# Inverse copies by rows, two local banks, planned slack for small matmuls, and a reordered first tile in a hybrid encoder step

## The chip, the cores and the metric

The kernel runs on one core of a Trainium2 chip. The metric is the device time of one execution in microseconds (us), as the median over several runs; lower is better. Five engines work side by side and meet at semaphores: TensorE (PE) multiplies matrices and loads its weights through PEld; VectorE (DVE), ScalarE (ACT) and GpSimd (POOL) do the elementwise work; SyncE (SP) issues the DMAs. PE writes its results into eight PSUM banks of 128x512 float32 numbers, and DVE and ACT read them from there.

## The reference

One layer of a hybrid encoder over 2048 prompt tokens and 32 sample tokens, width 1024. After a normalisation, a projection feeds two mixers; their outputs are projected back, and a feed-forward layer follows.

```
h = rmsnorm(x) * (1 + scale1) + shift1          # scale, shift, gate from silu(c) @ ada_w
p = h @ w_in                                    # columns: u, v | q, k, v | z | a, b
mixer A:  out = u * (W_s rmsnorm(v) + b_s)      # per chunk of 128 positions
mixer B:  gated delta rule, 4 heads x 128, in chunks:
    lmat = (kb k^T) * decay + I
    u_c, w_c = triangular_solve(lmat, ...)      # the inverse
    per chunk: v_new = u_c - w_c S;  o = qg S + attn v_new;  S = S * gl + kg^T v_new
x += gate1 * (concat(A, B) @ w_out)
x += gate2 * (relu(h2 @ w_up)^2 @ w_down);  y = rmsnorm(x)
```

## The kernel before

**A planner sets the order.** The kernel writes its operations into a list (`Program.op`), each with its engine, an estimated cost, and the operations that it must follow. `Program.schedule` then plays the list through: at each step the engine that is free first takes its best ready operation. What comes out is a fixed order for each engine; no time of the plan reaches the chip. Each engine works through its order and waits at semaphores where an operand is not there. Priorities go CHAIN, INV, LOCAL, EVAC, GEMM, IDLE. On PE everything but GEMM is small, and a dictionary `HOLD` lets GEMM matmuls pass a ready small one for a while: before the change LOCAL alone is held, by 1000 planned ns. Costs between engines are in `LATENCY`.

**Stages.** The tokens go in two halves of 1024 and 1056, each cut in groups of up to 512 columns. A projection tile (`gemm`) is 24 matmuls into one bank: eight slices of the contraction, each as three products (high by high, high by low, low by high parts of float32). The stages: `startup` (x is loaded, its sum of squares gives the row of inverse roots r, the modulation comes from `ada_first`, and h is made tile by tile for the first group while z is projected); then for each half `v_stage`, eight slabs of projection weights, with the delta rule beside them, and `u_stage`; then `out_stage` for both halves; then `feed_forward`.

**Banks.** `self.banks` gives tags to the eight banks: "g" (0, 1, 2) for projection tiles, "L" (3) for the local work of the delta rule, "C" (4, 5) for its chain over chunks, "B" (6) for the inverse, "M" (7) for sums, transposes and the gating mixer. The feed-forward part uses all eight as "f". Each use of a tag takes the next bank of its ring and must follow the last reader of that bank.

**The delta rule.** For each half and head, `delta_local` makes the matrices of each chunk pair (bank L), `delta_inv` the inverse: eight or ten small copies take the 16x16 diagonal blocks out to a DRAM tensor `nd_d`, one load brings them back in another shape, POOL inverts them all at once in 30 operations, two or four copies go through `ud_d`, and six sets of small matmuls (bank B) put the blocks together. `delta_chain` then walks over the chunks with two heads side by side; in each chunk PE works three times (`pa`, `px`, `pu`, bank C), with DVE or ACT between, and each step needs the one before.

**What the planner knows of the DRAM copies.** A view's region is that of the slice it was made from; `re(...)` keeps it. Before the change all copies into `nd_d` are views of `nd[:64]` rearranged, and so each overlaps the others and follows them in the plan, with `DMA_LATENCY` (3500 planned ns) between.

**The start.** In `startup`, `stats(0)` ends in `rms_row`: PE sums the squares into bank M, DVE and POOL take the power of -0.5, PE spreads the result over the partitions into bank M, and ACT copies it to a row in SBUF. Each first tile is then multiplied by the row (`h_value`; for every third k on POOL), scaled, split into BH and BL, and used. `consts` sets constants on POOL with `fill`.

Of the kernel before, what the change touches and what calls it, by code (L numbers as in the profile page):

```python
# [11 lines left out]
ALU = mybir.AluOpType  # L12
# [44 lines left out]

CHAIN, INV, LOCAL, EVAC, GEMM, IDLE = range(6)
TURN = 84
HOLD = {LOCAL: 1000}  # L60

# [133 lines left out]
def R(x):  # L195
    return x.ap if isinstance(x, View) else x
# [10 lines left out]
class Program:  # L207
# [37 lines left out]
    def schedule(self):  # L245
# [20 lines left out]
        def finish(i, start, end):  # L266
            o = ops[i]
            o.start = start
            order.append((start, i))
            for j in o.succ:  # L270
                s = ops[j]
                s.ready = max(s.ready, end + o.lat + LATENCY.get((o.eng, s.eng), 0.0))
                s.npred -= 1
                if s.npred == 0:
                    release(j, s.ready)
# [61 lines left out]
class Kern:  # L337
# [50 lines left out]
        e = self._e(eng)  # L388
        self.p.op(eng, c, lambda: e.tensor_copy(R(out), R(in_)), [out], [in_])

    def fill(self, out, value, eng=POOL):
        e = self._e(eng)
        self.p.op(eng, 100 + out.n, lambda: e.memset(R(out), value), [out], [])

    def transpose32(self, out, in_):
        nc = self.nc
# [152 lines left out]
    def setup(self):  # L549
# [108 lines left out]
    def startup(self):  # L658
        i, c = self.i, self.dma
        c(self.craw, i["cT"])  # L660
        self.act(self.cs, self.craw, AF.Silu)
        self.fill(self.ones, 1.0, DVE)
        self.fill(self.mhalf, -0.5, DVE)
        xr = [[8, 9, 10, 11], [4, 5, 7, 12]]
        x = [[self.slot(s, lo, (P, 512)) for s in xr[g] for lo in (0, HALF)] for g in range(2)]
        load = lambda g: [c(x[g][k], self.x_src(0)(k, 512 * g, 512)) for k in range(KT)]
        row = [self.row[:, 512 * g : 512 * g + 512] for g in range(2)]

        def stats(g):
# [12 lines left out]
        self.cp(self.nrm, k1[:, 96:120].re("p (n k) -> p n k", n=3))  # L682
        self.cp(self.ident, k1[:, 120:248])
        stats(0)
# [19 lines left out]
        self.consts()  # L704

    def consts(self):
        i = self.i
        ld = lambda v, src: self.dma(v, src, 4 * int(np.prod(v.shape)))
        bc = lambda v, n: self.dma(v, i[n].partition_broadcast(P))
        with self.p.at(GEMM):  # L710
            ld(self.wsT, i["wsT"])
            self.fill(self.wsT[64:128, :, 0:64], 0.0)
            bc(self.sgub, "sgub")
            bc(self.sgug, "sgug")
            ld(self.triu, i["triu"])
            ld(self.mask, i["mask"])
            ld(self.convw, i["convw"])
            ld(self.sconv, i["sconv"])
            ld(self.dngc, i["dngc"])
            bc(self.dtb, "dtb")  # L720
            bc(self.alog, "alog")
            for h in range(H):
                self.fill(self.S[h], 0.0)
            self.fill(self.halo, 0.0)
            self.fill(self.ab, 0.0)
            zero = self.slot(4, 0, (P, 1024))[:36]
            self.fill(zero, 0.0)
            for d in self.ud_d:
                self.dma(d.re("c a x -> (c a) x"), zero)
            self.fill(self.z0, 0.0)  # L730

            for x in self.r1s + self.vns + self.ofs:
                self.fill(x, 0.0)
            zero = self.slot(4, 0, (P, 384))
            self.fill(zero, 0.0)
# [116 lines left out]
        self.tt(bl, x, bh.f32(), ALU.subtract, eng)  # L852

    def h_value(self, hf, g, k, x, r, a, kind):
        self.tt(x, x, r, ALU.mult, POOL if k % 3 == 2 else DVE)
        for so, sw, q in segs(hf, g):
            s = slice(so, so + sw)
            c, b = a[:, k, q : q + 1], self.modc[:, kind, k, q : q + 1]
            if k % 4 == 1 and not kind:
                self.ts(x[:, s], x[:, s], c, ALU.mult, b, ALU.add, POOL)  # L860
            elif kind or k % 4 == 3:
                self.act(x[:, s], x[:, s], AF.Identity, scale=c, bias=b)
            else:
                self.ts(x[:, s], x[:, s], c, ALU.mult, b, ALU.add)
# [311 lines left out]
    def delta_inv(self, hf, h, nb):  # L1176
# [24 lines left out]
        ud_d = self.ud_d[self.nud % 2]  # L1201
        self.nud += 1
        for s in range(2):
            d = ud_d[:8].re("c a (s j t i) -> s t (c a) j i", s=2, j=16, t=2)
            self.dma(d[s, s], Uv[32 * s : 32 * s + 32])
            if hf == 1:
                d = ud_d[8:9, 0:1].re("c a (s j t i) -> s t (c a) j i", s=2, j=16, t=2)
                self.dma(d[s, s], Uv[64 + s : 65 + s])
# [448 lines left out]
    def put(self, ops, name, m, x):  # L1657
        ops.setdefault(name, {})[m] = self.operand(self.rp, x)
# [238 lines left out]
```

## Time and profile before

| | |
|---|---|
| median of 3 runs | 2337.24 us (2336.88 to 2339.47) |
| the profiled execution | 2330.84 us, of which the span 2328.8 us |
| granted TensorE clock | 0.998 |
| busy: PE, PEld | 98%, 93% of the span |
| busy: DVE, ACT, POOL | 71%, 53%, 26% |

The span goes from the first to the last instruction. An engine's busy time counts overlapping instructions once; a matmul's end is modelled, and one matmul begins before the one ahead of it has ended, so a PE that is busy may still begin its matmuls later than it could. The weight load (PEld) of a matmul stands in a row of its own, and a wait of PE for an operand shows there first.

### The profile page before, as it was taken

To read this page: it belongs to the slowest core of one execution; us is meant where nothing else is said; L and a number is where in the kernel's file an instruction comes from. 1 tells how busy PE (TensorE), PEld (TensorE's weight loads), DVE (VectorE), ACT (ScalarE), POOL (GpSimd) and SP (SyncE) were. 2 spreads that over 40 slices of the span, in tenths; PEclk is the share of its full clock that TensorE was granted. 3 is DMA by queue.
4 is the path that set the end of the run, shared out by engine and by line. 5 is a ranking of instruction groups with operands and counts; after the bars stand their busy time and mean duration, and the time that the engine had idled before them with its cause. 6 is when DMAs were issued, how large, how long until landed. Compare 5 with 4: busy or idle time off the path is not lost.

```text
span 2328.8 us, 45703 instructions
## 1 busy us (share of the span) xinstructions
PE 2292.2 (98%) x15906; PEld 2171.0 (93%) x15906; DVE 1653.2 (71%) x3651; ACT 1226.1 (53%) x2816; POOL 607.5 (26%) x830
## 2 busy tenths in 40 slices
PE   7999999999999999999999999999999999999998
PEld 4877879999999888999999999999999999999998
DVE  5557646667655546589999989776668886666775
ACT  5465546666655435376556555753344564334343
POOL 2235331332423323345544424200000250000001
PEclk9999999999999999999999999999999999999999
DMA  9789666657557767888777786997667797666771
GB/s 322 224 291 317 222 183 214 188 166 232 165 157 225 242 204 232 262 290 277 248 255 251 256 280 229 344 321 233 221 214 252 264 302 232 221 214 215 246 225 54
DMA packets 367247, 552.59 MB, mean 237 GB/s; under 512 B 70988, under 2 KB 191200, under 8 KB 367016
## 3 DMA queue, kind: packets, MB, share of 16 engines
q1 hardware_dynamic: 367016, 549.68, 72.5%
q8 instruction: 125, 2.05, 0.4%
q14 instruction: 106, 0.87, 0.1%
HBM read 395.25 MB, written 154.28 MB: 236 GB/s over the span
## 4 chain that ended last, share of the span: by engine, by line
PE 59%; DMA 3%; DVE 2%; issue 1%; ACT 1%; POOL 0%; SPq 0%; POOLq 0%; DVEq 0%; ACTq 0%
PE f L412 52%; PE g L412 6%; DMA s<-th_d 1%; PE C L412 1%; DVE s L366 1%; DVE s L371 1%; ACT s L351 0%; DVE BL L366 0%; DMA wh<-sd_d 0%; DVE wl L366 0%; POOL s L366 0%; DMA wr<-w_o 0%; PE B L412 0%; DMA th_d<-s 0%; ACT BH L351 0%
## 5 line engine op out<-in xcount | busy, mean ns | idle before, releaser
L351 ACT ACTIVATE s<-s 128x348 fp32r<-128x348 f32 (+13 forms) x1077 | 496.0, 483 | 341.3 <-DVE s L366 131.4
L412 PE MATMUL f<-s,wh 128*128 128x348 f32 (+1 forms) x2768 | 662.4, 322 | 0.4 <-DVE s L366 0.3
L412 PEld LDWEIGHTS f<-s,wh 128*128 128x128 f32 x2768 | 481.0, 188 | 2.2 <-DVE s L366 1.9
L366 DVE TENSOR_TENSOR s<-f,s 128x348 f32<-128x348 f32 (+1 forms) x696 | 349.6, 515 | 170.4 <-PE f L412 169.2
L412 PE MATMUL f<-s,wl 128*128 128x348 f32 (+1 forms) x1384 | 444.9, 321 | 0.0
L412 PE MATMUL g<-BH,wh 128*128 128x512 f32 (+2 forms) x1112 | 411.3, 370 | 0.0
L412 PE MATMUL g<-BH,wl 128*128 128x512 f32 (+2 forms) x1112 | 391.4, 352 | 0.0
L412 PE MATMUL g<-BL,wh 128*128 128x512 f32 (+2 forms) x1112 | 390.1, 351 | 0.0
L366 DVE TENSOR_TENSOR s<-s,s 128x348 fp32r<-128x348 f32 (+7 forms) x679 | 350.9, 546 | 45.7 <-POOL s L366 16.7
L412 PE MATMUL f<-BL,wh 128*128 128x348 f32 (+1 forms) x1024 | 330.2, 322 | 0.0
L412 PE MATMUL f<-BH,wh 128*128 128x348 f32 (+1 forms) x1024 | 329.3, 322 | 0.0
L412 PE MATMUL f<-BH,wl 128*128 128x348 f32 (+1 forms) x1024 | 328.7, 321 | 0.0
L351 ACT ACTIVATE wh<-s 128x512 fp32r<-128x512 f32 (+1 forms) x277 | 173.7, 634 | 232.0 <-PE f L412 190.6
L366 POOL TENSOR_TENSOR s<-s,s 128x512 f32<-128x512 f32 (+5 forms) x156 | 197.6, 1275 | 330.5 <-ACT s L351 163.4
L366 POOL TENSOR_TENSOR s<-s 64x39 f32<-64x39 f32 (+12 forms) x298 | 159.5, 535 | 444.0 <-issue 381.7
L412 PEld LDWEIGHTS f<-s,wl 128*128 128x128 f32 x1384 | 260.6, 188 | 0.0
L366 DVE TENSOR_TENSOR wl<-s,wh 128x512 fp32r<-128x512 f32 (+1 forms) x277 | 215.4, 786 | 35.7 <-ACT wh L351 34.6
L412 PEld LDWEIGHTS g<-BH,wh 128*128 128x128 f32 x1112 | 209.6, 188 | 22.7 <-issue 5.2
L412 PEld LDWEIGHTS g<-BH,wl 128*128 128x128 f32 x1112 | 208.9, 188 | 19.1
L412 PEld LDWEIGHTS g<-BL,wh 128*128 128x128 f32 x1112 | 210.0, 189 | 16.7 <-DVE BL L366 0.2
L371 DVE SCALAR_TENSOR_TENSOR s<-s,s,s 128x256 f32<-128x256 f32 (+5 forms) x318 | 164.2, 538 | 59.4 <-ACT s L351 34.2
L366 DVE TENSOR_TENSOR wl<-wr,wh 128x512 fp32r<-128x512 f32 (+2 forms) x164 | 159.1, 973 | 57.5 <-ACT wh L351 54.9
(116 smaller groups left out, 3328.0 us busy)
## 6 DMA issues: line engine op xcount, KB each, us to landing
s<-w_u SPq DMA_DIRECT2D x124, 256.0 KB
s<-w_d SPq DMA_DIRECT2D x121, 256.0 KB
wh<-su_d SPq DMA_DIRECT2D x114, 256.0 KB
wl<-su_d SPq DMA_DIRECT2D x114, 256.0 KB
wh<-sd_d SPq DMA_DIRECT2D x100, 256.0 KB
wl<-sd_d SPq DMA_DIRECT2D x100, 256.0 KB
wr<-w_b SPq DMA_DIRECT2D x42, 512.0 KB
s<-adaw SPq DMA_DIRECT2D x32, 512.0 KB
```

Of the source, the lines that this page charges most:

```text
L351: self.p.op(ACT, c, lambda: nc.scalar.activation(out=R(out), in_=R(in_), func=func, **{k: R(v) for k, v in kw.items()}), [out, accum], [in ...
L366: self.p.op(eng, c, lambda: e.tensor_tensor(out=R(out), in0=R(a), in1=R(b), op=op), [out], [a, b])
L371: self.p.op(DVE, c, lambda: nc.vector.scalar_tensor_tensor(out=R(out), in0=R(a), scalar=R(s), in1=R(b), op0=op0, op1=op1), [out], [a, s, b])
L412: nc.tensor.matmul(R(out), R(l), R(r), **kw)
```

## The change

Five edits. The copies into and out of the DRAM tensors of the inverse are written as slices of rows (and, for `ud_d`, of columns), so that the planner sees them as separate; they move the same numbers. Bank 2 goes from "g" to "L". The planner adds `SLACK`: a small PE operation (chain, inverse, local) whose operand comes from another engine is planned as ready 300 ns later; `HOLD` lets GEMM pass chain and inverse work for 300 planned ns. In the start, r of the first group stays in its bank M and is read from there by DVE (so no first tile is multiplied on POOL), and a power on POOL is run once ahead of its use. The fills of `consts` follow the last matmul of the first tiles. The first z tiles take banks "ggLL" in place of "gggL".

```diff
-HOLD = {LOCAL: 1000}
+SLACK = {CHAIN: 300, INV: 300, LOCAL: 300}
+HOLD = {CHAIN: 300, INV: 300, LOCAL: 1000}
...
-                s.ready = max(s.ready, end + o.lat + LATENCY.get((o.eng, s.eng), 0.0))
+                slack = SLACK.get(s.prio, 0.0) if s.eng == PE != o.eng else 0.0
+                s.ready = max(s.ready, end + o.lat + LATENCY.get((o.eng, s.eng), 0.0) + slack)
...
-        self.banks = {"g": [0, 1, 2], "L": [3], "C": [4, 5], "B": [6], "M": [7]}
+        self.banks = {"g": [0, 1], "L": [3, 2], "C": [4, 5], "B": [6], "M": [7]}
...
         self.fill(self.mhalf, -0.5, DVE)
+        self.tt(self.rcol[1], self.ones[:, :4], self.mhalf, ALU.pow, POOL)
...
-            self.rms_row([acc], 512, acc)
+            return self.rms_row([acc], 512, acc if g else None)
...
-        zs = [self.bank(t) for t in "gggL"]
+        zs = [self.bank(t) for t in "ggLL"]
         for k in range(KT):
             self.ada_first(k, ps[k % 2])
-            self.h_tile(0, 0, k, x[0][k], row[0], self.a1, 0)
+            self.h_tile(0, 0, k, x[0][k], r, self.a1, 0)
...
+        end = (len(self.p.ops) - 1,)
...
+        fill = lambda v, x: self.fill(v, x, after=after)
...
-        self.tt(x, x, r, ALU.mult, POOL if k % 3 == 2 else DVE)
+        self.tt(x, x, r, ALU.mult, POOL if k % 3 == 2 and not r.whole else DVE)
...
-        n16 = nd[:64].re("(s c a) (j i) -> s a j c i", s=2, c=8, j=16)
...
-                self.dma(n16[s, a], M[d, :, d])
+                self.dma(nd[32 * s + a : 32 * s + 32 : 4].re("c (j i) -> j c i", j=16), M[d, :, d])
...
-            d = ud_d[:8].re("c a (s j t i) -> s t (c a) j i", s=2, j=16, t=2)
-            self.dma(d[s, s], Uv[32 * s : 32 * s + 32])
+            put = lambda d, v: self.dma(d[:, :, 512 * s : 512 * s + 512].re("c a (j t i) -> t (c a) j i", j=16, t=2)[s], v)
+            put(ud_d[:8], Uv[32 * s : 32 * s + 32])
```

In the orders below a row is a line, an operation, what it writes and reads, the shape, and how many equal ones follow each other. The first place is SP's queue at the copies of the first inverse (`nd_d`, first half, head 0). Before:

```order
L404 DMA nd_d_0_163<-s_493 16x8x16
L404 DMA kq_d_99<-s_489 128x512
L404 DMA s_477<-v_d_102 128x256
L404 DMA pk_d_3_114<-s_475 128x768
L404 DMA h_d_161<-s_490 128x288
L404 DMA nd_d_0_163<-s_493 16x8x16
L404 DMA wr_96<-w_b 128x1024
```

Now:

```order
L406 DMA nd_d_0_163<-s_493 16x8x16 x8
L406 DMA pk_d_3_114<-s_475 128x768
L406 DMA s_477<-v_d_102 128x256 x2
L406 DMA s_476<-kq_d_98 128x2x256
L406 DMA wr_96<-w_b 128x1024
L406 DMA s_472<-nd_d_0_163 64x256
```

The eight copies, which stood some four issues apart, now stand in one run, and the load back follows behind five others.

The second place is PE in the chain of the second half, between two steps of one chunk (C rows read the state or the chain's operands; g rows are projection matmuls, here of the first half's out stage). Before:

```order
L412 MATMUL C_10100<-s_482,s_470 128x128 x2
L412 MATMUL g_9989<-BH_73,wh 128x512
L412 MATMUL g_9989<-BL_81,wh 128x512
L412 MATMUL g_9989<-BH_73,wl 128x512
L412 MATMUL g_9989<-BH_74,wh 128x512
L412 MATMUL g_9989<-BL_82,wh 128x512
L412 MATMUL g_9989<-BH_74,wl 128x512
L412 MATMUL C_10124<-s_483,s_471 128x128 x4
```

Now:

```order
L414 MATMUL C_9954<-s_482,s_470 128x128
L414 MATMUL g_9922<-BH_73,wh 128x512
L414 MATMUL g_9922<-BL_81,wh 128x512
L414 MATMUL g_9922<-BH_73,wl 128x512
L414 MATMUL g_9922<-BH_74,wh 128x512
L414 MATMUL g_9922<-BL_82,wh 128x512
L414 MATMUL g_9922<-BH_74,wl 128x512
L414 MATMUL g_9922<-BH_75,wh 128x512
L414 MATMUL g_9922<-BL_83,wh 128x512
L414 MATMUL g_9922<-BH_75,wl 128x512
L414 MATMUL C_9974<-s_482,s_469 128x128 x2
```

Six projection matmuls between two steps have become nine here. Over the whole order up to the feed-forward part, 3 or 6 stand between two C rows 65 times before and 21 times now, 9 to 15 of them 30 times before and 71 times now. The change of tag from one PE row to the next falls from 610 to 555 times, and of these the returns to a g row from 253 to 237. The last C row stands after 3627 of 4176 projection matmuls before, and after 3537 now; the last inverse row after 3309, and after 3084 now.

The third place is DVE at the first tiles (s_477 to s_480 are the x tiles, C the banks of the modulation, s_493 the row r in SBUF, M_555 the bank that holds r now). Before:

```order
L366 TENSOR_TENSOR modc<-C_503,s_482 128x2x2
L366 TENSOR_TENSOR s_477<-s_477,s_493 128x512
L366 TENSOR_TENSOR modc<-C_503,modc 128x2x2 x3
L380 TENSOR_SCALAR a_89<-modc,nrm 128x2
L380 TENSOR_SCALAR s_477<-s_477,a_89,modc 128x512
L366 TENSOR_TENSOR modc<-C_504,s_482 128x2x2
L366 TENSOR_TENSOR s_477<-s_477,s_493 128x512
L366 TENSOR_TENSOR modc<-C_504,modc 128x2x2
L366 TENSOR_TENSOR s_478<-s_478,s_493 128x512
L366 TENSOR_TENSOR BL_79<-s_477,BH_71 128x512
```

Now:

```order
L368 TENSOR_TENSOR s_477<-s_477,M_555 128x512
L368 TENSOR_TENSOR modc<-C_503,s_482 128x2x2
L368 TENSOR_TENSOR s_477<-s_477,M_555 128x512
L368 TENSOR_TENSOR modc<-C_503,modc 128x2x2
L368 TENSOR_TENSOR s_478<-s_478,M_555 128x512
L368 TENSOR_TENSOR modc<-C_503,modc 128x2x2
L368 TENSOR_TENSOR s_478<-s_478,M_555 128x512
L368 TENSOR_TENSOR modc<-C_503,modc 128x2x2
L368 TENSOR_TENSOR s_479<-s_479,M_555 128x512
L382 TENSOR_SCALAR a_89<-modc,nrm 128x2
L368 TENSOR_TENSOR s_479<-s_479,M_555 128x512
L382 TENSOR_SCALAR s_477<-s_477,a_89,modc 128x512
```

Six multiplications by r stand ahead of the first scaling, where one stood; two more, the second high-low split of weights (wl) and two sums stand between it and the first BL now. On PE the transposes of the third modulation slice (C_503) now stand ahead of the first g row; before, six g rows stood ahead of them.

More of the change, by code (lines that the diff above doesn't have):

```diff
@@ L389, in cp, with fill @@
         self.p.op(eng, c, lambda: e.tensor_copy(R(out), R(in_)), [out], [in_])
-    def fill(self, out, value, eng=POOL):
+    def fill(self, out, value, eng=POOL, after=()):
         e = self._e(eng)
-        self.p.op(eng, 100 + out.n, lambda: e.memset(R(out), value), [out], [])
+        self.p.op(eng, 100 + out.n, lambda: e.memset(R(out), value), [out], [], after=after)
     def transpose32(self, out, in_):
@@ L683, in startup @@
         self.cp(self.ident, k1[:, 120:248])
-        stats(0)
+        r = stats(0)
         self.sq = self.slab_list()
@@ L703, in startup, with consts @@
         self.next_slab()
-        self.consts()
-    def consts(self):
+        self.consts(end)
+    def consts(self, after):
         i = self.i
         ld = lambda v, src: self.dma(v, src, 4 * int(np.prod(v.shape)))
+        fill = lambda v, x: self.fill(v, x, after=after)
         bc = lambda v, n: self.dma(v, i[n].partition_broadcast(P))
@@ L711, in consts @@
             ld(self.wsT, i["wsT"])
-            self.fill(self.wsT[64:128, :, 0:64], 0.0)
+            fill(self.wsT[64:128, :, 0:64], 0.0)
             bc(self.sgub, "sgub")
@@ L722, in consts @@
             for h in range(H):
-                self.fill(self.S[h], 0.0)
-            self.fill(self.halo, 0.0)
-            self.fill(self.ab, 0.0)
+                fill(self.S[h], 0.0)
+            fill(self.halo, 0.0)
+            fill(self.ab, 0.0)
             zero = self.slot(4, 0, (P, 1024))[:36]
-            self.fill(zero, 0.0)
+            fill(zero, 0.0)
             for d in self.ud_d:
                 self.dma(d.re("c a x -> (c a) x"), zero)
-            self.fill(self.z0, 0.0)
+            fill(self.z0, 0.0)
             for x in self.r1s + self.vns + self.ofs:
-                self.fill(x, 0.0)
+                fill(x, 0.0)
             zero = self.slot(4, 0, (P, 384))
-            self.fill(zero, 0.0)
+            fill(zero, 0.0)
             for h in range(H):
@@ L1203, in delta_inv @@
         for s in range(2):
-            d = ud_d[:8].re("c a (s j t i) -> s t (c a) j i", s=2, j=16, t=2)
-            self.dma(d[s, s], Uv[32 * s : 32 * s + 32])
+            put = lambda d, v: self.dma(d[:, :, 512 * s : 512 * s + 512].re("c a (j t i) -> t (c a) j i", j=16, t=2)[s], v)
+            put(ud_d[:8], Uv[32 * s : 32 * s + 32])
             if hf == 1:
-                d = ud_d[8:9, 0:1].re("c a (s j t i) -> s t (c a) j i", s=2, j=16, t=2)
-                self.dma(d[s, s], Uv[64 + s : 65 + s])
+                put(ud_d[8:9, 0:1], Uv[64 + s : 65 + s])
         ud, td = self.new("ud"), self.new("td")
```

## The prediction

> **What bounds the kernel now.** I read the page and the busy times of three stretches (start, mixers with the out stage, feed-forward) first.
>
> ```profile
> span 2328.8 us, 45703 instructions
> 0.00:58.00 58.00, 41.86 (x266) 25.11 (x267) 34.92 (x84) 29.11 (x47) 13.96 (x25) 1.00 0.91 323
> 58.00:1015.00 957.00, 947.70 (x7461) 848.00 (x7460) 580.16 (x1598) 523.65 (x1374) 311.01 (x590) 1.00 0.71 223
> 1015.00:2329.00 1314.00, 1302.69 (x8184) 1297.85 (x8182) 1038.15 (x1970) 673.32 (x1397) 282.54 (x216) 1.00 0.74 244
> ```
>
> After each stretch come its length, the busy time of PE, PEld, DVE, ACT and POOL, the granted clock, the DMA share and GB/s. PE is busy for 947.70 of 957 us in the mixers and for 1302.69 of 1314 in the feed-forward part. So the time is PE's work plus small losses, and an engine that merely gets faster beside it pays nothing. In the feed-forward part no PE work has a priority that the change touches; I take it as unchanged. What the planner can win lies in the 957 us, in waits of small matmuls. So the second view is what PE's weight load waited for there, and the third the same for the matmuls (us in total, times, longest):
>
> ```profile
> PEld B L412 <- issue: 14.8, 45, 1.4
> PEld C L412 <- DVE s L371: 7.1, 19, 0.7
> PEld C L412 <- ACT s L351: 1.0, 3, 0.5
> PEld B L412 <- DVE s L397: 1.6, 2, 1.2
> PEld B L412 <- DVE s L371: 0.7, 3, 0.3
> PE C L412 <- DVE s L371: 2.1, 8, 0.3
> PE B L412 <- DVE s L397: 0.8, 1, 0.8
> ```
>
> The largest row, "issue", waits for no operand, and the change has no hold on it. Next comes a chain matmul (C) that waits for DVE: 7.1 us at the load, only 2.1 at the matmul, because the matmul ahead still counts as busy. The fourth view, the timeline, shows which figure is nearer the loss:
>
> ```profile
> 838.14 0.48 PE L412 MATMUL g<-BH,wh 128*128 128x512 f32 x1
> 838.46 0.40 PE L412 MATMUL g<-BL,wh 128*128 128x512 f32 x1
> 838.69 0.40 PE L412 MATMUL g<-BH,wl 128*128 128x512 f32 x1
> 851.42 0.40 PE L412 MATMUL g<-BH,wl 128*128 128x512 f32 x1
> 852.09 0.71 PE L412 MATMUL C<-s,s 128*128 128x128 f32 x4 [0.27 <-DVE s L371]
> 851.29 0.74 DVE L371 SCALAR_TENSOR_TENSOR s<-C,s,s 128x128 f32<-128x128 f32 x2 [0.69 <-ACT s L351]
> ```
>
> In a steady run a matmul begins 0.23 us after the one ahead (838.46, 838.69). The chain matmul at 852.09 begins 0.67 us after its predecessor: a loss of 0.44, of which 0.27 shows as idle. DVE ended its two updates at 852.03. Six g matmuls, 1.4 us, had been planned here, and 0.4 us more were needed.
>
> **Planned slack: a gain.** The rows that end on DVE or ACT come to 7.1 + 1.0 + 1.6 + 0.7 = 10.4 us at the load, and 2.9 at the matmul. How much remains, the order says: 3 or 6 g matmuls stood between C rows 65 times, and now 21 times; 9 to 15 have taken their place. Nine give 0.7 us more than six, where the example lacked 0.4. So I leave 21/65, a third, of the waits: the gain is 2/3 of 10.4, 6.9 us; at least 2/3 of 2.9, 1.9; at most 10.4. The example's loss exceeds its idle time, so I take 6.9.
>
> **Fewer returns: a gain.** The first g matmul behind a small one holds PE for 0.32 us (838.14 to 838.46), 0.09 over the steady 0.23. The returns fall from 253 to 237, and 16 x 0.09 = 1.4 us; bounds 0 and 1.4.
>
> **Inverse copies: nothing by themselves.** Now they run like this, the last line being the chain's transposes, with the time of the first and the last:
>
> ```profile
> 251.33 0.34 SPq L404 DMA_DIRECT2D nd_d<-s  x1
> 254.21 0.54 SPq L404 DMA_DIRECT2D nd_d<-s  x1
> 280.05 0.49 SPq L404 DMA_DIRECT2D s<-nd_d  x1
> L423 PE MATMUL C<-ident,s x68: 270/272/329, 399.8 to 921.2; 128*128 128x128 f32 x68
> ```
>
> From first copy to load back pass 28.7 us. In one run, at some 0.45 us an issue, eight take 3.6 us and a landing; an inverse can begin about 20 us earlier. PE has g work meanwhile, so nothing is saved, but it covers the slack: three steps per chunk, each up to 0.6 us later (300 + 300 planned ns), over 9 chunks and two pairs of heads, are 32 us in the second half. Without the earlier inverses the last C rows, at 921.2, would move into the second half's out stage and hold it up. By the order the last C row comes 90 g matmuls, or 90 x 0.23 = 21 us, earlier. SP issues the eight in one piece of 3.6 us, with the projection weights behind them; those waits lay between the copies before, so I put no cost there.
>
> **Two banks for g: a loss.** A tile's reader may be one tile late now, not two. The gating part has the tightest place I found:
>
> ```profile
> 101.85 0.28 PE L412 MATMUL g<-wl,BH 128*128 128x260 f32 x1
> 101.96 0.28 PE L412 MATMUL g<-wh,BH 128*128 128x260 f32 x1
> 101.33 1.06 ACT L351 ACTIVATE wh<-wr 128x1024 fp32r<-128x1024 f32 x1 [1.63 <-PE g L412]
> 102.41 1.28 ACT L351 ACT_TABLE_LOAD   x1
> 105.28 0.66 ACT L351 ACTIVATE s<-g 128x256 f32<-128x256 f32 x2
> L351 ACT ACTIVATE s<-g 128x512 f32<-128x512 f32 x39 | 23.3, 597 | 26.9 <-PE g L412 26.1 <-POOL s L366 0.6
> L351 ACT ACTIVATE s<-g,s 128x512 f32<-128x512 f32 x24 | 16.5, 688 | 0.0
> L371 DVE SCALAR_TENSOR_TENSOR s<-s,s,s 128x512 f32<-128x512 f32 x72 | 60.6, 842 | 26.7 <-ACT s L351 25.6
> ```
>
> ACT reads two waiting tiles at 105.28, having been taken by a weight split and table loads since 101.33: 3.95 us, where a tile of 24 matmuls at 0.12 lasts 2.9. With two banks PE would lose about 1.1 us. Elsewhere a 512-column tile lasts 24 x 0.23 = 5.6 us and its two readings take 0.60 + 0.69. I count one such place in each half, and allow up to five: 1.5 us taken, bounds 0 and 5.5. [...]
>
> **The start: about even.** Rows of the first tiles:
>
> ```profile
> 14.20 1.89 PE L412 MATMUL C<-s,s 128*2 128x256 f32 x16
> 14.55 1.93 POOL L366 TENSOR_TENSOR rcol<-rcol,mhalf 128x4 f32<-128x4 f32 x1 [12.99 <-DVE rcol L380]
> 57.86 1.03 POOL L366 TENSOR_TENSOR rcol<-rcol,mhalf 128x4 f32<-128x4 f32 x1 [0.25 <-DMA s<-dtb]
> 17.69 0.60 ACT L351 ACTIVATE s<-M 128x512 f32<-128x512 f32 x1 [1.15 <-PE M L423]
> 18.32 0.69 DVE L366 TENSOR_TENSOR s<-s,s 128x512 f32<-128x512 f32 x1
> 20.20 1.45 DVE L380 TENSOR_SCALAR s<-s,a,modc 128x512 f32<-128x512 f32 x1
> 27.71 0.55 DVE L380 TENSOR_SCALAR s<-s,a,modc 128x512 f32<-128x512 f32 x1
> 22.91 0.68 DVE L366 TENSOR_TENSOR BL<-s,BH 128x512 fp32r<-128x512 f32 x1
> 23.30 0.50 PE L412 MATMUL g<-BH,wh 128*128 128x512 f32 x1
> 38.40 0.61 PE L412 MATMUL C<-s,s 128*2 128x256 f32 x8 [0.48 <-DMA s<-ada]
> L366 DVE TENSOR_TENSOR s<-M,s 128x512 f32<-128x512 f32 x16 | 11.0, 688 | 5.7 <-PE M L412 5.6
> ```
>
> The power falls from 1.93 to 1.03, but PE holds modulation matmuls until 16.09, so the spreading starts only about 0.45 earlier; the copy of 0.60 goes too. DVE begins near 17.3, a microsecond before 18.32. It then does six multiplications of some 0.6 us ahead of the first scaling, which POOL no longer slows (1.45 at 20.20, 0.55 at 27.71), and two more and a split before the first BL: near 24.4, not 22.91. In exchange later tiles find theirs done. The last slices of the modulation come at the DMA's pace (0.91 of the start, the wait at 38.40), so little of either sign reaches the end. I take a loss of 0.5; bounds a gain of 1.5 (PE's earlier start and the copy) and a loss of 2 (the first BL, and 0.5 for DVE's longer list). The late fills leave POOL beside DVE and cost nothing, since PE waits for none. [...]
>
> **Sum.** -6.9 - 1.4 + 1.5 + 0.5 = -6.3 us: the profiled execution's 2330.84 would become 2324.5. The runs shown have a median of 2337.24, 6.4 above it, so I carry the difference over: 2337.24 - 6.3 = 2330.9, **2331 us**. The bounds, all together, would be -13.3 and +5.6; half of this spread on each side gives 2327 to 2337 as the forecast's own range.
>
> **Rivals.**
>
> 1. *The waits only move.* If steps lack more than 0.7 us, or if B and g matmuls wait in the chain's place, only the lower 1.9 and half the returns remain: -1.9 - 0.7 + 1.5 + 0.5 = -0.6, 2336.6. For it: only 8 of 19 waits show as idle. Against it: the one measured in full lacked 0.4. Chance 0.21.
> 2. *All of it comes.* Every counted wait goes, no bank waits, the start gains: -10.4 - 1.4 - 1.5 = -13.3, 2324. For it: many steps have 12 or 15 g matmuls. Chance 0.16.
> 3. *Slower: two banks gate the q, k, v tiles.* ACT's copy out of a bank needs one of two raw buffers, which DVE frees after three updates of 0.84; if DVE is late by more than a tile, PE waits at each of the 60 such tiles (12 times 2 and 3 groups). At 0.27 each, the wait at 852.09, that is 16 us: -6.9 - 1.4 + 0.5 + 16.2 = +8.4, 2345.6. It decides from the point where ACT's reading ends over 5.6 us behind a tile's last matmul. Against it: three updates are 2.5 us of 5.6, and DVE is busy for 580 of 957 us. Chance 0.13.
> 4. *The edits don't do what they say* is out for the copies, which the order shows in one run; for the slack it is rival 1.
>
> **Chances.** The forecast has 0.50. A measurement of this kernel tells about 0.2%, 4.7 us, from no change, so faster means under 2332.6 and slower over 2341.9. Two thirds of the forecast (0.34) and rival 2 (0.16) are faster: 0.50, with 0.01 from the others 0.51. Rival 3 gives slower 0.11, and 0.01 more comes from a bad start: 0.12. The rest, 0.37, is no change. The range must hold 8 in 10: from 2322, below which lies a third of rival 2, to 2343, above which lies most of rival 3.
>
> **What would show it.** Right, if C's load waits on DVE fall from 7.1 to near 2.5 us, PE's idle time in the mixers falls by some 3 us, the last C row ends near 900, and the feed-forward part keeps its 1314 us. Wrong, if the g tag gets waits for ACT or DVE of over 5 us together (rival 3), if the first z tiles end over 2 us later than now, or if the feed-forward part changes by more than 1 us, which no term here covers.

## The result, and the profile after

| | before | after |
|---|---|---|
| median, us | 2337.99 (10 runs, 2335.88 to 2345.42) | 2331.64 (10 runs, 2328.59 to 2333.43) |
| ratio | 1 | 0.9968, 95% interval 0.9959 to 0.9978 |
| profiled execution, us (its span) | 2330.84 (2328.8) | 2331.24 (2329.5) |

The change makes the kernel 0.32% faster, some 7 us. The two profiled executions don't show it: the one of before was faster than any of the ten timed runs beside it, while the one of after lies at its median. So the profile of after is read here against a second profile of before as well, whose execution took 2337.06 us (the first experiment).

The mixers with the out stage in the profile after, from 58 us to its first feed-forward matmul (length, then busy time of PE, PEld, DVE, ACT and POOL, clock, DMA share, GB/s):

```profile
58.00:1009.70 951.70, 942.57 (x7457) 848.50 (x7456) 583.58 (x1596) 518.08 (x1370) 309.61 (x595) 1.00 0.71 224
```

The same stretch in the second profile of before, and in the first:

```profile
58.00:1017.90 959.90, 947.64 (x7459) 848.27 (x7458) 579.86 (x1597) 523.66 (x1373) 309.07 (x590) 1.00 0.71 222
58.00:1013.20 955.20, 946.41 (x7454) 847.00 (x7453) 578.43 (x1594) 522.25 (x1371) 309.95 (x589) 1.00 0.71 223
```

The rows hold the same work, 7454 to 7459 matmuls, so the lengths can be compared. Against the second profile of before the mixers with the out stage are 8.2 us shorter. PE's idle time gives 3.1 of it (959.90 - 947.64 = 12.3 against 951.70 - 942.57 = 9.1), and 5.1 lies inside the time that counts as busy. The prediction's example had shown that a late operand costs more than the idle time beside it, because the matmul ahead still counts as busy. Against the first profile they are only 3.5 us shorter, all of it inside the busy time: PE's idle time there was 955.20 - 946.41 = 8.8. Two executions of one kernel thus differ by 4.7 us in this stretch. How much the change gains is told by the medians; the rows are read for where it lies.

What PE's weight load waited for from 58 to 1015 us, after (us in total, times, longest); the last row is the matmuls' own view of the third:

```profile
PEld B L414 <- issue: 12.0, 38, 0.4
PEld g L414 <- ACT s L353: 3.9, 4, 1.4
PEld C L414 <- DVE s L373: 3.4, 7, 0.9
PEld C L414 <- ACT s L353: 0.8, 1, 0.8
PEld B L414 <- DVE s L373: 0.6, 2, 0.4
PE C L414 <- DVE s L373: 1.6, 3, 0.6
```

Of the weight load's rows that the prediction shows, two differ in the second profile of before; C's 19 waits for DVE (7.1 us), C's for ACT and the last of B's are the same there:

```profile
PEld B L412 <- issue: 16.8, 47, 1.9
PEld B L412 <- DVE s L397: 1.5, 1, 1.5
```

The reader is to see three things. Chain matmuls that wait for DVE fell from 19 to 7. Matmuls of g wait for ACT now, in a row that before doesn't have. And the small matmuls of the inverse have fewer of the gaps that wait for nothing, a row on which the prediction counted no gain.

The sum over all tiles, from 58 us to the first feed-forward matmul, tells a fourth. The waits of the weight load for an operand come to 23.9 and 25.6 us in the two profiles of before, and to 25.0 after. What C and B lost there, g's waits for ACT and B's waits for one DMA (4.8 us, before 2.3 and 1.6) have for the most part taken up. The waits for nothing fell from 20.2 and 22.4 us to 14.2.

The copies in the timeline after (start, duration):

```profile
238.15 3.73 SPq L406 DMA_DIRECT2D nd_d<-s  x8
245.50 0.49 SPq L406 DMA_DIRECT2D s<-nd_d  x1
```

The chain's last transposes, in the view of the C tiles (shortest, median and longest in ns, then first and last start); then, in the timeline, the first BL of the start, and the place where the prediction expected two banks to bind, with the two that are like it:

```profile
L425 PE MATMUL C<-ident,s x84: 270/272/475, 17.3 to 897.6; 128*128 128x128 f32 x84
```

```profile
24.72 0.68 DVE L368 TENSOR_TENSOR BL<-s,BH 128x512 fp32r<-128x512 f32 x1
105.68 0.66 ACT L353 ACTIVATE s<-g 128x256 f32<-128x256 f32 x2
106.47 0.19 PEld L414 LDWEIGHTS g<-wh,BH 128*128 128x128 f32 x1 [0.86 <-ACT s L353]
199.39 0.19 PEld L414 LDWEIGHTS g<-BH,wh 128*128 128x128 f32 x1 [0.86 <-ACT s L353]
459.40 0.19 PEld L414 LDWEIGHTS g<-wh,BH 128*128 128x128 f32 x1 [1.36 <-ACT s L353]
```

The eight copies go in one piece of 3.73 us, and the load back follows 7.35 us behind the first copy instead of 28.7. The last chain transposes start at 897.6 us, not 921.2. Three weight loads of g wait until ACT has read a tile, as where a bank is not yet free; they add up to 3.1 us, and the first is at the place that the prediction named.

### The profile page after: what moved, and what is told of

Same layout as the page of the kernel before. It is cut to its first block, busy times and chain, and to the rows that moved or that the text cites. A ratio compares the mean times of both kernels' runs of the same rounds, so it can differ in the third digit from the quotient of the medians.

```text
span 2329.5 us, 45687 instructions
## 1 busy us (share of the span) xinstructions
PE 2288.9 (98%) x15906; PEld 2172.3 (93%) x15906; DVE 1661.6 (71%) x3653; ACT 1220.8 (52%) x2813; POOL 605.1 (26%) x829
## 5 line engine op out<-in xcount | busy, mean ns | idle before, releaser
L353 ACT ACTIVATE s<-s 128x348 fp32r<-128x348 f32 (+14 forms) x1077 | 494.6, 482 | 338.4 <-DVE s L368 136.0
L414 PE MATMUL f<-s,wh 128*128 128x348 f32 (+1 forms) x2768 | 663.4, 322 | 1.1 <-DVE s L368 0.7
L414 PEld LDWEIGHTS f<-s,wh 128*128 128x128 f32 x2768 | 481.0, 188 | 4.4 <-DVE s L368 3.3
L414 PE MATMUL f<-s,wl 128*128 128x348 f32 (+1 forms) x1384 | 444.7, 321 | 0.0
L414 PE MATMUL g<-BH,wh 128*128 128x384 f32 (+2 forms) x1104 | 408.2, 370 | 0.0
L414 PE MATMUL g<-BH,wl 128*128 128x384 f32 (+2 forms) x1104 | 388.2, 352 | 0.0
L414 PE MATMUL g<-BL,wh 128*128 128x384 f32 (+2 forms) x1104 | 387.1, 351 | 0.0
L368 DVE TENSOR_TENSOR s<-s,s 128x348 fp32r<-128x348 f32 (+9 forms) x673 | 349.2, 547 | 47.5 <-ACT s L353 21.7
L414 PE MATMUL f<-BL,wh 128*128 128x348 f32 (+1 forms) x1024 | 330.3, 323 | 0.5 <-DVE BL L368 0.5
L414 PE MATMUL f<-BH,wh 128*128 128x348 f32 (+1 forms) x1024 | 329.3, 322 | 1.4 <-DVE s L373 1.4
L414 PE MATMUL f<-BH,wl 128*128 128x348 f32 (+1 forms) x1024 | 328.6, 321 | 0.0
L368 POOL TENSOR_TENSOR s<-s,s 128x512 f32<-128x512 f32 (+5 forms) x154 | 191.6, 1253 | 303.1 <-ACT s L353 137.8
L414 PEld LDWEIGHTS f<-s,wl 128*128 128x128 f32 x1384 | 260.5, 188 | 0.0
L414 PEld LDWEIGHTS g<-BH,wh 128*128 128x128 f32 x1104 | 208.1, 189 | 21.1 <-issue 3.9
L414 PEld LDWEIGHTS g<-BH,wl 128*128 128x128 f32 x1104 | 207.4, 188 | 19.0
L414 PEld LDWEIGHTS g<-BL,wh 128*128 128x128 f32 x1104 | 208.5, 189 | 16.0
L353 ACT ACTIVATE wh<-wr 128x512 fp32r<-128x512 f32 (+2 forms) x164 | 130.4, 796 | 129.0 <-PE f L414 58.4
```

The source lines that it names most:

```text
L353: self.p.op(ACT, c, lambda: nc.scalar.activation(out=R(out), in_=R(in_), func=func, **{k: R(v) for k, v in kw.items()}), [out, accum], [in ...
L368: self.p.op(eng, c, lambda: e.tensor_tensor(out=R(out), in0=R(a), in1=R(b), op=op), [out], [a, b])
L414: nc.tensor.matmul(R(out), R(l), R(r), **kw)
```

## The experiments

All ran beside runs of before whose medians were 2340.1 to 2340.9 us. Ratios are to those, with their 95% intervals; the change's own 0.9968 is to the runs beside it, with 2337.99 us. In kernels whose source has the slack's lines, also with slack 0, the lines of the helpers are two higher (L414 for L412). In the diffs three dots stand for further lines.

| kernel | median, us | ratio | interval |
|---|---|---|---|
| before again | 2341.79 | 1.0000 | 0.9989 to 1.0012 |
| copies | 2337.12 | 0.9988 | 0.9976 to 1.0001 |
| banks | 2342.60 | 1.0013 | 1.0000 to 1.0025 |
| start | 2356.35 | 1.0060 | 1.0047 to 1.0073 |
| late fills (part of the start) | 2339.88 | 0.9993 | 0.9984 to 1.0003 |
| slack | 2356.74 | 1.0067 | 1.0050 to 1.0083 |
| copies, banks | 2343.81 | 1.0017 | 1.0004 to 1.0031 |
| copies, banks, start | 2344.23 | 1.0013 | 1.0000 to 1.0025 |
| slack, copies | 2334.91 | 0.9972 | 0.9958 to 0.9987 |
| slack, copies, banks | 2335.43 | 0.9978 | 0.9968 to 0.9988 |
| slack, copies, start | 2335.16 | 0.9975 | 0.9965 to 0.9986 |
| the change with slack 600 | 2330.64 | 0.9954 | 0.9939 to 0.9968 |

### Before again

No edit.

> The kernel before, unchanged, profiled a second time. The profile of before on record was one of 2330.84 us, below each of its ten timed runs (2335.88 to 2345.42), and between the two profiles on record only 3.5 us are gained up to the first feed-forward matmul (1013.2 to 1009.7 us) and 4 us are given back in the feed-forward part. Theory A (the profile of before was a lucky execution): this profile's execution is at 2336 to 2339, and its first feed-forward matmul comes at 1016 to 1019 us, so the change gains 6 to 8 us in the mixers. Theory B (the mixers gain 3.5 us, the rest lies in the feed-forward part): the first feed-forward matmul stays at 1013 and the rest of the span is some 4 us longer than in the first profile. The ratio to before is 1.000 within 0.001.

It agrees with before, and gave the second profile used above.

### The change without its start

The whole change except the late fills, the row read in its bank and the early power.

```diff
...
-            self.h_tile(0, 0, k, x[0][k], r, self.a1, 0)
+            self.h_tile(0, 0, k, x[0][k], row[0], self.a1, 0)
...
```

> Copies by rows, two local banks and the slack on the kernel before, with its old start. By the prediction the start costs 0.5 us, so this gains 6.8 us (ratio 0.9971) and the first z tile begins at 23.3 us as before. Rival: the start is the part that gains, and this gains under 3 us (ratio over 0.9987).

It measured 0.9978. The whole change has 0.9968, and the intervals overlap: within the combination the new start gains 0.1% by the ratios, and that it gains at all isn't shown.

### The slack alone, and with the copies

The slack alone, on before:

```diff
-HOLD = {LOCAL: 1000}
+SLACK = {CHAIN: 300, INV: 300, LOCAL: 300}
+HOLD = {CHAIN: 300, INV: 300, LOCAL: 1000}
...
```

The edit has two parts, the later planned time (`SLACK`) and the longer hold (`HOLD`). They always ran together; "slack" means both.

> The slack and the longer hold alone, with three g banks, one local bank and the copies seen as one chain. By the prediction the waits go as before (-6.9) and the returns (-1.4), but the cover of the earlier inverses is missing: the chain is up to 32 us later in the second half and its last C rows reach the second half's out stage, so the gain is smaller than with the copies: between -5 and +20 us (ratio 0.998 to 1.009). Rival: the chain has room in any case and this alone gains 7 us or more (ratio 0.997 or less).

It lost 0.67%, inside the bounds that were set. The chain ran into the second half's out stage, which starts at 897.6 us in this profile. Below are the stretch ahead of the stage and its first 300 g matmuls, then the last chain transposes, then the two longest waits of PE:

```profile
58.00:897.60 839.60, 834.34 (x6746) 741.13 (x6746) 503.28 (x1426) 470.13 (x1249) 262.99 (x549) 1.00 0.69 216
897.60:982.40 84.80, 69.10 (x428) 65.00 (x426) 44.35 (x116) 33.52 (x83) 25.05 (x24) 0.92 0.69 212
```

```profile
L425 PE MATMUL C<-ident,s x84: 270/273/448, 17.6 to 952.3; 128*128 128x128 f32 x84
```

```profile
951.88 0.82 PE L425 MATMUL C<-ident,s 128*128 128x128 f32 x2 [3.36 <-DVE s L368]
960.72 0.61 PE L414 MATMUL g<-BH,wh 128*128 128x288 f32 x1 [8.01 <-ACT BH L353]
```

Up to the out stage only 5.3 us of 839.60 are idle. In the out stage it is 15.7 of 84.8: chain steps stand there with little g work between them, and the g matmuls wait for tiles that the chain's end holds up. That is how the two long waits are read here; it was not tested apart. The last transposes stand 54.7 us inside the stage; in the second profile of before it is 5.7 us, where the same 300 g matmuls take 50.50 us:

```profile
919.60:970.10 50.50, 50.34 (x316) 49.95 (x315) 29.64 (x56) 22.21 (x40) 20.38 (x20) 1.00 0.81 258
```

```profile
L423 PE MATMUL C<-ident,s x84: 269/273/422, 17.4 to 925.3; 128*128 128x128 f32 x84
```

With the copies by rows added to the slack:

```diff
-                self.dma(n16[s, a], M[d, :, d])
+                self.dma(nd[32 * s + a : 32 * s + 32 : 4].re("c (j i) -> j c i", j=16), M[d, :, d])
...
```

> Slack with the copies by rows, three g banks, old start. By end of chain: the last C row stands at g matmul 3741, still 141 behind the beginning of the out stage, so most of the loss of the slack alone stays: 2348 to 2358 us. By the prediction, where the earlier inverses are the cover of the slack: 2331 to 2337 us, as with all three edits.

```profile
905.90:966.80 60.90, 56.83 (x349) 54.62 (x348) 34.71 (x78) 24.84 (x52) 22.86 (x22) 0.97 0.79 244
L425 PE MATMUL C<-ident,s x84: 270/272/421, 17.4 to 936.1; 128*128 128x128 f32 x84
```

The first row has the same 300 g matmuls of the out stage. That part of the stage shrinks from 84.80 to 60.90 us, of which 4.1 are idle, and the kernel is 22 us faster than with the slack alone. The last transposes still stand 30.2 us inside the stage, so the chain's end need not clear it. The copies are the slack's cover, as the prediction has it; the other theory, by which the place of the last C row in the order sets the time, asked for 2348 to 2358 us and falls.

### The copies, the banks, and both

The copies as above; the banks:

```diff
-        self.banks = {"g": [0, 1, 2], "L": [3], "C": [4, 5], "B": [6], "M": [7]}
+        self.banks = {"g": [0, 1], "L": [3, 2], "C": [4, 5], "B": [6], "M": [7]}
...
```

> Only the inverse copies by rows. Two theories of the ladder so far. By end of chain, the time follows the place of the last C row in PE's order, counted in g matmuls; the second half's out stage begins at g matmul 3600. Before has it at 3627 (2340 us on this chip), the start alone at 3693 (2356), the slack alone at 3780 (2357), the copies, banks and slack together at 3537 (2335). Here it stands at 3534, so the chain is out of the out stage: 2331 to 2336 us. By single waits, as the prediction has it, copies gain nothing by themselves since PE has g work meanwhile: 2337 to 2342 us, as before.

> Only the second local bank, taken from the three g banks. By end of chain: the last C row stands at g matmul 3534 as with the copies alone, because local matmuls no longer hold each other up and the chain is planned earlier: 2331 to 2338 us (g waits on ACT of 1 to 4 us included). By the prediction's term, two g banks cost 0 to 5.5 us and gain nothing: 2340 to 2346 us.

> Copies and banks, no slack, old start: beside the run with the slack too (2335.4) this gives the worth of the slack where the chain has room. By end of chain: the last C row stands at 3438, before the out stage, so the chain costs nothing here; without the slack the C load waits on DVE stay near 7 us: by the prediction's slack term of 6.9 us, 2342 us; if the slack is worth nothing and the room is all, 2333 to 2336 us.

The copies alone are within what can be told from nothing (-0.12%), the banks alone cost 0.13%, at the edge of what can be told, both together 0.17%. On top of the copies the banks thus cost 0.29%, with intervals that do not meet. The end-of-chain theory wanted a gain from each and has none. The chain's and g's waits from 58 to 1040 us in the kernel with both:

```profile
PEld C L412 <- DVE s L371: 10.8, 22, 1.4
PEld g L412 <- ACT s L351: 5.2, 5, 1.6
```

Beside it stands the same kernel with the slack too, the change without its start (its row from 58 to 1015 us):

```profile
PEld C L414 <- DVE s L373: 3.2, 7, 1.2
```

The C waits are 3.2 us in place of 10.8, and the ratio is 0.9978 in place of 1.0017, with intervals that do not meet. That is the slack's worth where the chain has cover: 0.39%, 9 us.

### The start alone, and its late fills alone

```diff
+        self.tt(self.rcol[1], self.ones[:, :4], self.mhalf, ALU.pow, POOL)
...
-            self.h_tile(0, 0, k, x[0][k], row[0], self.a1, 0)
+            self.h_tile(0, 0, k, x[0][k], r, self.a1, 0)
...
+        end = (len(self.p.ops) - 1,)
...
+        fill = lambda v, x: self.fill(v, x, after=after)
...
```

> The new start alone (r in its bank, late fills, a power ahead) on the kernel before. By the prediction +0.5 us, between -1.5 and +2 (ratio 0.9994 to 1.0009), with the first BL some 1.5 us later and the lead lost by the end of the z tiles. Rival: the new order of everything behind it moves the time by more than 2 us either way.

It lost 0.6%, 14 us. The prediction's term did not have it; the rival, more than 2 us either way, had it without sign or size. The first tiles are not the place. What the weight load waited for from 58 to 1040 us; then, in the timeline, the costliest of these places, what ACT did ahead of it and PE's rows; then two stretches there:

```profile
PEld C L412 <- DVE s L371: 10.7, 24, 1.5
PEld L L412 <- ACT s L351: 3.3, 4, 2.2
PEld L L423 <- ACT s L351: 1.4, 2, 1.1
```

```profile
365.06 1.28 ACT L351 ACT_TABLE_LOAD   x1
368.69 1.78 ACT L351 ACTIVATE BH<-s 128x288 fp32r<-128x288 f32 x5
373.75 0.60 ACT L351 ACTIVATE s<-L,s 128x128 f32<-128x128 f32 x2
374.40 1.93 PE L412 MATMUL L<-s 128*128 128x256 f32 x4 [2.00 <-ACT s L351]
377.55 0.66 PE L423 MATMUL L<-ident,s 128*128 128x128 f32 x2 [1.21 <-issue]
```

```profile
360.00:380.00 20.00, 16.08 (x114) 14.55 (x113) 13.76 (x39) 15.38 (x42) 4.15 (x11) 0.86 0.68 186
380.00:400.00 20.00, 20.00 (x329) 18.54 (x328) 9.93 (x34) 8.87 (x34) 3.64 (x5) 0.79 0.31 96
```

ACT works without a break from 365 to 374 us, behind a table load; the local matmuls that need its last result stand next in PE's order, and PE idles for 2.00 us, 300 us after the start. Behind it the granted clock falls to 0.86 and 0.79 in two stretches of 20 us, which is 2 x (0.14 + 0.21) x 20 = 14 us at half the clock. PE is idle for 1.9 of them, so some 6 us of work are lost there, on top of the waits. The planner has put the local rows too close behind ACT there, without any slack.

Then the late fills alone, without the row read in its bank and the early power:

```diff
...
-            self.fill(self.wsT[64:128, :, 0:64], 0.0)
+            fill(self.wsT[64:128, :, 0:64], 0.0)
...
```

> Of the new start only the late fills; the row of inverse roots is copied as before. PE's order is that of before. If the loss of the start alone comes from the rows that were planned in another order behind it (the L rows that wait for ACT at 374 us, the C rows on DVE), it is gone here: 2338 to 2343 us, as before. If the fills themselves hold POOL up later, it stays: 2350 to 2357 us.

It took 2339.88 us, no change. Its PE order is that of before, operation for operation. So the fills are not the loss. The order behind the start differs where the row is read in its bank; that part and the early power were not run alone, and a re-planned order as the cause is the reading of the waits above.

### The change with three g banks, without slack, with double slack

The change with its banks put back:

```diff
-        self.banks = {"g": [0, 1], "L": [3, 2], "C": [4, 5], "B": [6], "M": [7]}
+        self.banks = {"g": [0, 1, 2], "L": [3], "C": [4, 5], "B": [6], "M": [7]}
...
```

> The change with its banks put back: g on three banks, one local bank; copies, slack and start as in the change. By the bank term (the banks alone measured 0.13% slower, on top of slack and copies 0.06%): 1 to 3 us faster than the change, 2329 to 2333 us where before stands at 2340, with the g waits on ACT of 3.9 us gone. If the second local bank is what lets the start and the slack go together, the loss of the start alone (0.6%) shows again: 2345 to 2355 us.

It has 0.9975, the change 0.9968: neither theory's gain or loss is seen. The waits of g for a tile that ACT reads fall from 3.9 to 0.9 us, but the chain ends later. The first 300 g matmuls of its out stage, which take 49.90 us in the change, the last transposes, and g's waits from 58 to 1040 us:

```profile
910.80:970.30 59.50, 55.22 (x350) 53.44 (x349) 34.76 (x78) 24.91 (x52) 22.58 (x22) 1.00 0.79 244
```

```profile
L425 PE MATMUL C<-ident,s x84: 270/272/477, 17.4 to 940.4; 128*128 128x128 f32 x84
```

```profile
PEld g L414 <- ACT BH L353: 2.0, 1, 2.0
PEld g L414 <- ACT s L353: 0.9, 1, 0.9
```

The change without its slack:

```diff
-SLACK = {CHAIN: 300, INV: 300, LOCAL: 300}
+SLACK = {CHAIN: 0, INV: 0, LOCAL: 0}
-HOLD = {CHAIN: 300, INV: 300, LOCAL: 1000}
+HOLD = {LOCAL: 1000}
```

> The change with slack 0 and the old hold: copies, banks and start. By the slack term (6.9 us in the prediction; 0.39%, 9 us, between the runs with copies and banks, with and without it): 2338 to 2344 us, C load waits on DVE near 10 us. If the start always costs its 0.6% where there is no slack: 2352 to 2360 us. If the gain of the change came from the copies and the start: 2331 to 2335 us.

It took 2344.23 us, 1.0013: all of the gain is gone, and the C waits from 58 to 1040 us are back:

```profile
PEld C L414 <- DVE s L373: 9.1, 20, 1.6
```

Over all tiles, up to the first feed-forward matmul, the waits for an operand are 35.1 us, where the change has 25.0, and those for nothing 18.9, where it has 14.2. The start does not always cost 0.6%: with copies and banks and no slack it costs nothing (1.0013 with it, 1.0017 without).

The change with slack 600 in place of 300 for all three kinds:

```diff
-SLACK = {CHAIN: 300, INV: 300, LOCAL: 300}
+SLACK = {CHAIN: 600, INV: 600, LOCAL: 600}
```

> The change with slack 600 in place of 300. If the waits that are left (3.4 us of C on DVE) are the same ones a longer slack covers: C waits on DVE under 2 us and 2328 to 2333 us. If the chain then runs out of cover (its last C row stands 36 g matmuls later, at 3573, still before the out stage at 3600), or the longer slack only makes PE idle: 2334 to 2345 us.

```profile
PEld C L414 <- DVE s L373: 1.3, 3, 0.7
```

```profile
58.00:1008.70 950.70, 943.13 (x7460) 849.34 (x7459) 586.68 (x1597) 515.57 (x1370) 310.00 (x600) 1.00 0.71 224
```

The first row is the chain's waits from 58 to 1040 us, the second the stretch up to its first feed-forward matmul. The chain's waits more than halve once more, and the median is 2330.64 us. No loss is seen beside the change, and the intervals (0.9939 to 0.9968 and 0.9959 to 0.9978) overlap: that it beats the change isn't shown. The hold is the same in both, so the planned time by itself acts on the chain's waits.

## Why the prediction was right, step by step

The forecast was 2331 us, the measured median is 2331.64, and the rivals fell. That is not because every term had its size.

**Slack, -6.9 us: right in kind, and it is the whole gain; the size is partly luck.** Taken out of the change it costs 0.45% (0.9968 against 1.0013), out of the change without its start 0.39%; 9 to 10.5 us. The prediction counted the waits that the kernel before shows, 10.4 us, and those rows fell by 5.6 us, to 3.4 + 0.8 + 0.6 = 4.8. But other tiles' waits took their place, so the sum over all tiles is that of before, and PE's idle time, which was to fall by some 3 us, did so against the second profile of before and not against the first. The slack removes the waits that the other edits bring (copies and banks without it have C waits of 10.8 us, not 7.1) and some that wait for nothing. So it is worth more than the step had, and more than the 8.3 us of this step and the returns together. The other edits cost more, too: banks and start were priced at 2.0 us, and the change without its slack stands 3 us over before, with an interval that begins at none. In the sum the two errors cancel. On the copies alone the slack gained less, 0.9988 to 0.9972, with intervals that overlap. Of the chain's own 7.1 us it left 3.4, about half, where the step left a third.

**Inverse copies, nothing but the cover: right, but for the place of the chain's end.** Alone -0.12%, with an interval that holds zero; without them the slack loses 0.67% in the out stage. The last C row was to end near 900 us, and its last transposes start at 897.6. The step gave that to the copies alone. The second local bank makes as much: with slack, copies and start the transposes start at 940.4 us on three g banks, and at 897.6 on two. And the chain may end inside the out stage: with slack and copies it does, by 30.2 us, and the gain is there (0.9972).

**Two g banks, +1.5 us: within its bounds, for one reason too few.** They cost 0.13% alone, 3 us, 0.29% on top of the copies, and nothing that can be told in the change. They were not the costliest edit: the start alone cost 0.60%. The waits for ACT came where the step put them, 3.9 us in all, under the 5 us of the slower rival. What the step missed is the second local bank as a gain: the first 300 g matmuls of the out stage take 49.90 us, where three g banks make it 59.50. With the slack the two cancel over the whole kernel.

**The start, +0.5 us: its size can't be told within the change, wrong alone.** The first BL came at 24.72 us, where the step said 24.4; the first z matmul starts at 25.3 us, 2.0 later than in the profile of before on record and 0.8 later than in its second one. The first z tiles end at 57.9 us, between 57.5 and 58.3 in the two, so the delay is made good, as the step said. Reading r in its bank cost DVE nothing: the eight multiplications took 677 ns in the mean, and those of before from SBUF 684. One premise failed, the power that was to fall from 1.93 us to 1.03:

```profile
1.08 1.01 POOL L368 TENSOR_TENSOR rcol<-ones,mhalf 128x4 f32<-128x4 f32 x1 [0.65 <-DVE mhalf L395]
14.40 1.94 POOL L368 TENSOR_TENSOR rcol<-rcol,mhalf 128x4 f32<-128x4 f32 x1 [12.31 <-DVE rcol L382]
```

The early power, the first of the kernel, took 1.01, and the one that counts took 1.94 behind it; so the 1.93 was not the price of being first, and running a power early saved nothing. What makes it slow stays open. Within the change the start gains 0.1% by the ratios, with intervals that overlap. Alone it lost 14 us. The step priced the moved work and not the new plan behind it, which, as its waits are read above, put local and chain rows 300 us and more further on close behind ACT and DVE.

**Issue, "the change has no hold on it": failed.** The row of inverse matmuls that wait for no operand went from 14.8 and 16.8 in two profiles of before to 12.0. In the other kernels it lies between these. The four lowest, 12.0 to 12.7, all have slack and copies, and none without slack is under 13.5; but the slack alone has 14.6, and the change with three g banks 15.1. Why stays open.

**Fewer returns, -1.4 us: not tested apart.** The time that left PE's counted busy time, 5.1 us or 3.8 by the profile of before that is taken, holds it, if it came.

**The feed-forward part "keeps its 1314 us", or at most 1 us of change: failed as a test.** From the first to the last feed-forward matmul pass 1302.9 us in the profile of before on record, 1304.3 in its second one and 1306.9 after. PE's order there is the same in both kernels, and the late fills alone, with PE's order of before throughout, have 1306.9. So single executions differ by 4 us there without a change in PE's order, and a bound of 1 us on one execution could not test it. The longest of the waits after:

```profile
PE f L414 <- DVE s L373: 1.4, 1, 1.4
```

**Rivals.** That the waits only move was to give 2336.6 us; the time and the run without slack refute it, though in part they did move. That two banks gate the q, k, v tiles is refuted by g's three long waits, none of which lies among sixty such tiles as a series. That all of it comes would have been 2324 us; double slack came to 2330.64.

## What to carry to other kernels

A plan made on exact durations puts small dependent matmuls just behind their operands, and every operand that is a little late stops the engine that sets the time (here the chain's 19 waits for DVE, 7.1 us): here some planned slack ahead of them was worth more than any edit of the work itself. Slack makes a chain longer (alone it moved the last chain transposes from 925.3 to 952.3 us), so it needs cover; here the same slack lost 0.67% without the edits that start the chain earlier and gained with them. And where a planner orders everything from one list, an edit at the start can cost its time hundreds of microseconds later (here in the wait that ended at 374.40 us), so edits are to be measured together as well as one by one.

## What was not expected of the hardware

Behind an idle of PE of 1.37 us the granted clock fell to half, and that cost more than the idle itself. The place, in the timeline of the kernel with copies and banks, and stretches of one microsecond around it (length, then PE's busy time; the clock is third from the end):

```profile
723.75 0.82 PE L412 MATMUL B<-s,s 32*32 32x32 f32 x48 [1.37 <-DVE s L380]
```

```profile
722.00:723.00 1.00, 0.38 (x3) 0.07 (x1) 0.68 (x2) 1.00 (x6) 0.00 (x0) 1.00 0.23 46
723.00:724.00 1.00, 0.25 (x12) 0.25 (x15) 0.96 (x3) 1.00 (x7) 0.00 (x0) 1.00 0.84 263
724.00:725.00 1.00, 1.00 (x48) 0.96 (x46) 0.97 (x2) 1.00 (x4) 0.00 (x0) 1.00 0.66 229
725.00:726.00 1.00, 1.00 (x7) 1.00 (x6) 0.96 (x4) 0.03 (x1) 0.00 (x0) 0.78 0.14 45
728.00:729.00 1.00, 1.00 (x10) 0.90 (x9) 0.63 (x3) 0.60 (x2) 0.00 (x0) 0.52 0.87 243
729.00:730.00 1.00, 1.00 (x14) 0.93 (x14) 0.34 (x1) 0.00 (x0) 0.31 (x1) 1.00 0.79 291
```

PE is full again at 724 us, and only then the clock falls to half, from about 725.6 to 729.0 (0.78 in one microsecond is 0.44 us at half): 3.4 us, in which by an estimate half, 1.7 us of work, is lost on top of the wait of 1.37. What the estimate rests on is the pace of the g matmuls in the profile after. Where its clock is 0.50, from 24.4 to 27.8 us, two of 512 columns begin 0.43 us apart, and where it is 1.00 again, 0.23:

```profile
25.84 0.63 PE L414 MATMUL g<-BL,wh 128*128 128x512 f32 x1
26.27 0.63 PE L414 MATMUL g<-BH,wl 128*128 128x512 f32 x1
28.60 0.39 PE L414 MATMUL g<-BL,wh 128*128 128x512 f32 x1
28.83 0.39 PE L414 MATMUL g<-BH,wl 128*128 128x512 f32 x1
```

After the change's own wait of 1.4 us in the feed-forward part the clock stays full, as these two rows show, and for the rest of that part one row from 1384 to 2316.6 us, with 1.00:

```profile
1384.00:1385.00 1.00, 0.00 (x0) 0.00 (x0) 1.00 (x3) 0.00 (x0) 1.00 (x1) 1.00 0.67 227
1386.00:1387.00 1.00, 1.00 (x8) 1.00 (x7) 1.00 (x3) 0.00 (x0) 0.00 (x0) 1.00 0.04 13
```

Four other places, by rows of one microsecond, lie between 372 and 1464 us. In the change without its start PE is idle for 1.26 us in all from 1457 to 1459 us, and the clock is at half for 3.4 us from about 1460.1 (0.53, 0.50, 0.50 and 0.76 in the four microseconds from 1460). With slack and copies PE is idle for 1.69 us from 944 to 947 us, and the clock is at half for 3.4 us from about 947.4 (0.70, 0.50, 0.50, 0.59). In the start alone a wait of 2.00 us ended at 374.40, and the clock was at half from about 374.6 to 388.2, for 13.6 us, with two more gaps of PE in them. In the slack alone a wait of 3.36 us ended at 951.88, and the clock was at half from about 951.2, still inside it, to 964.9, for 13.7 us.

So the length of the idle time alone doesn't decide: 1.26 us in all and a single wait of 1.37 us were followed by half the clock, and the change's 1.39 us in three microseconds, in the same feed-forward part as the 1.26, were not. What decides stays open.

Part of the loss of the start alone is of this kind, some 6 us. Of the 13.7 us in the slack alone PE was idle for 8.7, so some 2.5 us of work were lost. The executions of these two had mean clocks of 0.992 to 0.995, those of before beside them 0.995 to 0.999.
